# Keeping the split halves of dense weights in DRAM: a hybrid decoder layer on one Trainium2 core

## Chip, cores and metric

The kernel runs on one core of one Trainium2 chip, in one launch. The metric is device time in microseconds (us), the median of several runs. All arithmetic is in float32; TensorE's operands are in the fp32r form, a rounded float32.

## What is computed

One layer of a decoder, for a prompt of 2048 tokens and for 8 sequences of 8 new tokens each (64 rows, "the sample"), with D = 1024. Cut to what matters here:

```
ada  = silu(c) @ w_ada + b_ada                      # 6 vectors of D: shifts, scales, gates
h    = rmsnorm(x) * (1 + sc_m) + sh_m
proj = h @ w_in                                      # D x 3584
rq, rk, rv, rg, sq, sk, sv = split(proj)             # 512 columns each
ro   = retention(rotary(rq), rotary(rk), rv), normed, * silu(rg)   # 4 heads of 128
so   = stick_breaking(sq, [past k | sk], [past v | sv]), normed    # 8 heads of 64
x    = x + g_m * (concat(ro, so) @ w_out)            # 1024 x 1024
h    = rmsnorm(x) * (1 + sc_f) + sh_f
a    = h @ w_up_gate ; b = h @ w_up_val              # D x 2816 each
ff   = (silu(causal_conv3(a)) * b) @ w_down          # 2816 x D
y    = rmsnorm(x + g_f * ff)
```

The sample attends to 2048 past tokens, whose keys and values lie in pages of 128 rows, found through a page table. Outputs are y, the new keys and values, the retention states and the last rows of the convolution.

## The kernel before

**Products in halves.** A float32 operand s is written as hi + lo: hi is s rounded to fp32r, lo is the remainder. A product of two such operands is three matmuls, hi x hi, hi x lo and lo x hi (`mm3`, L293 to L297). The pair of halves is made by `split` (L173): ScalarE (ACT) casts to hi, VectorE (DVE) subtracts hi from the source. This is done for weights and for activations.

**Blocks.** The prompt goes in four blocks of 512 tokens (g = 0 to 3). Each block needs all dense weights: the input projection in `in_block` (L607), the output projection in `out_block` (L1204), the MLP in `ffn_block` (L1268). The 64 sample rows ride with block 0 in the input projection and with block 3 after it, where products are 576 columns wide, in two pieces of 288.

**Weights.** Weights come in two ways. `w_fm` (L272) loads 256 columns of all 1024 rows (1 MiB, rows of 1 KiB) into a buffer called raw, for products that leave features on the partitions; it yields two pairs of halves. `w_tm` (L288) loads four tiles of 128 rows by 512 columns (1 MiB, rows of 2 KiB) through `w_rows` (L278), for products that leave tokens on the partitions; it too yields two pairs per load. Each half is a tile whl of 128 x 1024 (512 KiB). There are two raw buffers (L241) and six whl buffers, so three pairs (L242). Every block loads and splits all weights anew: 54 loads and 102 pairs in each block, 28 pairs for the input projection, 8 for the output projection, 66 for the MLP. The modulation `ada` (L504) uses the same pools for w_ada, once: 48 pairs.

**Order.** The code is written as generators, whose steps `_weave` (L138) interleaves: first the input projection of the blocks beside the modulation's rest and the decode attention of the sample (L1463), then the last input projections beside retention and block 0's attention (L1468), then output projections and MLPs of blocks 0 to 2 beside the attention of blocks 1 to 3 (L1496), and at last block 3's MLP alone (L1499). A scheduler turns this into one list of instructions for each engine, which the engine runs in order. SyncE (SP) issues every transfer, in its own order, so a transfer whose buffer isn't free yet holds back those behind it. Among them are the decode pages (L777 to L786: a page number is read into a register, then 256 KiB are loaded), the keys, queries and values that the projections write to DRAM and the attention reads back, and the outputs.

**Tiles that the text names.** whl: halves of weights; raw: weights as loaded; act: normalised activations as features, in halves; d and z: sums in PSUM; hf: scratch rows; st, kf, vst: results on their way to DRAM; page, khl, vhl: decode pages and their halves; abe, aom, ahl: attention weights; sbr: the scale of the attention's norm. L159 is the helper `tt` (a binary operation of two tensors), L165 the helper `dma`, L174 the cast in `split`. L454 transposes the scales of the attention's norm for PE.

Of the kernel before, what the change touches and what calls it, by code (L numbers as in the profile page):

```python
# [5 lines left out]
F32 = mybir.dt.float32  # L6
F32R = mybir.dt.float32r
# [112 lines left out]
class _Stream:  # L120
    """Traced work in steps; each step yields its share of the whole, or None while it has to wait."""

# [15 lines left out]
def _weave(streams, until=None):  # L138
    """Traces the streams side by side, each at the rate that lets all of them end together."""
    while any(s.live for s in streams) and (until is None or until.live):  # L140
        for s in sorted((s for s in streams if s.live), key=lambda s: s.got / s.total):
            if s.step():
                break
        else:
            raise RuntimeError("streams wait for each other")


def body(tc, I, O):
# [18 lines left out]
    def ld(o, i):  # L167
        dma(sp, o, i)
# [7 lines left out]

    w_in, w_out = I["w_in"][0], I["w_out"][0]
    w_ug, w_uv, w_dn = I["w_up_gate"][0], I["w_up_val"][0], I["w_down"][0]
    xp = I["x_prompt"][0]
# [84 lines left out]

    # ------------------------------------------------------------ weights
    def w_split(src, a, b, eng=dve):
# [4 lines left out]

    def w_fm(src, c0):  # L272
        raw = T(wraw, [P, 2048], F32, "raw").rearrange("p (a b) -> p a b", a=8)
        ld(raw, src[:, c0 : c0 + 256].rearrange("(k p) c -> p k c", p=P))
        for m in range(2):
            yield w_split(raw[:, :, m * P : (m + 1) * P], 8, P)

# [9 lines left out]

    def w_tm(src, r0, n, c0):  # L288
        for r, raw in w_rows(src, r0, n, c0):
            for q in range(0, raw.shape[1], 2):  # L290
                yield r + q, w_split(raw[:, q : q + 2], 2, 512)

# [6 lines left out]
    def tok_mm(ps, x, w, start, stop):  # L299
        """Rows of tokens x (hi, lo) times w; a short tile has hi and lo side by side, their rows to be added."""  # L300
        if isinstance(x, tuple):
            mm3(ps, x, w, start, stop)
        else:
            pe.matmul(ps, x, w[0], start=start, stop=False)  # L304
            pe.matmul(ps, x, w[1], start=False, stop=stop)  # L305
# [40 lines left out]
    def by_tile(tiles, k0, n):  # L346
        """The products of two rows of weights with the tiles; those of the last two tile after tile."""
        order = [(k, tile) for k in range(k0, k0 + 2) for tile in tiles]
        return sorted(order, key=lambda kt: kt[1]) if k0 == n - 2 else order

    def dense_pair(wts, acts, t, features=False):
        """Two tiles of outputs, the first half of the tokens (or features) of both before the second."""
        outs = [fm_banks(t) for _ in wts]
        for h in range(2):
            for wt, out in zip(wts, outs):
                if features:
                    for ps, c0, c1 in out:
                        fm_chunk(wt, acts, ps[:, : c1 - c0], c0, c1, range(h * 4, h * 4 + 4))
                elif t == 512:
                    fm_chunk(wt, acts, out[0][0][:, h * 256 : h * 256 + 256], h * 256, h * 256 + 256)  # L360
                else:
                    ps, c0, c1 = out[h]
                    fm_chunk(wt, acts, ps[:, : c1 - c0], c0, c1)
        return outs
# [7 lines left out]

    # ------------------------------------------------------------ norms
    def rstd_of(ss, n, scale, p=P):
# [21 lines left out]
    def half_features(x, o, n, kh, A, B, acts, hpool):  # L396
        """Half kh of the columns of normalised rows, scaled and shifted, into columns o.. as hi and lo."""
        ks = slice(kh * 4, kh * 4 + 4)
# [32 lines left out]
    def sb_norm(o, n, pl, gain, tag):  # L431
        """o: [P, n], two heads of 64 rows; returns o / rms of its head * gain. Yields between its steps."""
        w = min(P, n)
# [29 lines left out]

    # ------------------------------------------------------------ preparation
    def prep(pl, kp):
# [100 lines left out]

    # ------------------------------------------------------------ input projection
    def raw_features(hp, xT):
        """The first block's rows, normalised and transposed before the modulation is known."""
        for i, o, n in TILES + [(NT, TB, NS)]:  # L570
# [179 lines left out]

    # ------------------------------------------------------------ decode attention
    def decode(dp):
# [184 lines left out]

    # ------------------------------------------------------------ retention
    def group_norm(ps, gg, qd, pl, n):
        """ps: [n, 512], four heads, each lacking its rows' decay qd; returns the gated norm of the whole."""  # L940
        mv = T(pl, [P, HR, 2], F32, "mv")
# [155 lines left out]

    # ------------------------------------------------------------ prompt attention
    def attention(blocks, tp):
# [102 lines left out]

    # ------------------------------------------------------------ output projection and MLP
    def out_block(g, xpools, fp, samp):  # L1204
        """Output projection, residual and the MLP's normalised input; xpools() gives the pool of x2."""
        t = TB + (NS if samp else 0)
# [61 lines left out]
    def ffn_block(g, x2, fp, samp, after=None):  # L1268
        """The MLP and the final norm; `after` runs between the halves of the last down projection."""
        t = TB + (NS if samp else 0)  # L1270
# [123 lines left out]
    def conv_state(fi, fp):  # L1394
        """The last rows of two tiles of gates, as rows."""
        s = T(fp, [P, 512], F32, "hf")
        ps = pz()
        for q in range(2):
            cs = T(fp, [P, 18], F32, "cvc")
            pool.tensor_copy(cs[:, 0:2], carry[:, fi + q, :])  # L1400
            pool.tensor_copy(cs[:, 2:18], scarry[:, fi + q].rearrange("p b j -> p (b j)"))
            pe.transpose(ps[:18, q * P : (q + 1) * P], cs, ident)
        act.copy(s[:18, : 2 * P], ps[:18, : 2 * P])
        cs = slice(fi * P, (fi + 2) * P)
        sv(O["conv_state_prompt"][:, cs], s[0:2, : 2 * P])
        sv(O["conv_state_sample"].rearrange("b j d -> (b j) d")[:, cs], s[2:18, : 2 * P])
# [12 lines left out]

    # ------------------------------------------------------------ the parts in their order  # L1420
    tile_pool = lambda name, bufs=1: tc.tile_pool(name=name, bufs=bufs, reuse_waits="tile")
# [85 lines left out]
class _Bufs:  # L1507
    """A pool whose tags have their own numbers of slots."""

# [9 lines left out]
class _Two:  # L1519
    """Two pools, the first for the tags given."""  # L1520

# [44 lines left out]
```

## Time and profile before

| | |
|---|---|
| median of 3 runs | 3483.96 us (3482.68 to 3484.57) |
| span of the profiled execution | 3483.6 us |
| instructions | 49,595 |
| moved by DMA | 527.72 MB, 151 GB/s on average |
| read from and written to HBM | 442.47 MB and 81.99 MB |

The profile shows one execution, so its span stands for that execution's time. PE is TensorE's matmul queue and PEld its loads of stationary weights, which overlap; a matmul's duration reaches into the next one's, since they are pipelined. A row of groups reads: line, engine, operation, tile written <- tiles read, sizes, count | busy us, mean ns of one | idle us of the engine just before, and what ended it. A row of waits reads: who waited <- for whom: us in total, times, the longest. A row of stages gives the stage, its length, the busy time of each engine with its count of instructions, the clock granted to PE, the busy share of the 16 DMA engines and the rate.

### The profile page before, as it was taken

The page shows a single profiled execution, that of the slowest core. Times are in us where ns is not written, and L with a number is a line of the kernel's source. Part 1 is how long each engine was busy: PE and PEld are TensorE (multiplying, and loading weights), DVE is VectorE, ACT ScalarE, POOL GpSimd, SP SyncE. Part 2 cuts the span into 40 slices and gives each one's busy share as a digit, 9 for nine tenths or more (in the row PEclk, how much of TensorE's full clock was granted, in tenths as well). Part 3 has the DMA queues.
Part 4 walks back from the last instruction along what each step waited for, and adds up shares of the span by engine and source line. Part 5 has one row for each costly group of instructions (what it writes and reads, how often), then busy time and mean ns, then how long its engine had stood idle before and what let it go on. Part 6 is the DMA issues. An engine that isn't in the chain of part 4 may idle for free. (4 is left out here: it accounts for less than half of the span.)

```text
span 3483.6 us, 49595 instructions
## 1 busy us (share of the span) xinstructions
PE 3298.8 (95%) x17111; PEld 2693.4 (77%) x17111; DVE 2287.1 (66%) x3258; ACT 1777.9 (51%) x3153; POOL 1021.5 (29%) x1898
## 2 busy tenths in 40 slices
PE   7999999899999989999998999998899999899998
PEld 5887877776777768777877778777677777799997
DVE  5466666665665567777768777776877775545445
ACT  5457666554544456455556555554655553433323
POOL 3012011101433243434344333333433323221113
PEclk8999999999999989999999999999999999999999
DMA  6666776666756763443453333335333334332221
GB/s 226 229 198 193 234 230 218 221 223 211 210 178 194 246 196 103 121 121 112 121 182 118 118 118 112 106 112 181 109 118 106 112 103 136 112 107 88 83 86 65
DMA packets 406233, 527.72 MB, mean 151 GB/s; under 512 B 27830, under 2 KB 244009, under 8 KB 405982
## 3 DMA queue, kind: packets, MB, share of 16 engines
q1 hardware_dynamic: 405982, 524.55, 47.8%
q8 instruction: 136, 2.23, 0.3%
q14 instruction: 115, 0.94, 0.1%
HBM read 442.47 MB, written 81.99 MB: 151 GB/s over the span
## 5 line engine op out<-in xcount | busy, mean ns | idle before, releaser
L159 DVE TENSOR_TENSOR whl<-raw,whl 128x1024 fp32r<-128x1024 f32 x456 | 572.7, 1260 | 566.8 <-ACT whl L174 556.5
L174 ACT CAST whl<-raw 128x1024 fp32r<-128x1024 f32 x456 | 477.3, 1050 | 909.2 <-PE d L296 639.0
L295 PE MATMUL d<-act,whl 128*128 128x512 f32 (+2 forms) x2016 | 741.9, 369 | 5.5 <-ACT act L424 4.7
L297 PE MATMUL d<-act,whl 128*128 128x512 f32 (+2 forms) x2016 | 737.9, 366 | 4.6 <-DVE whl L159 4.6
L296 PE MATMUL d<-act,whl 128*128 128x512 f32 (+2 forms) x2016 | 735.7, 365 | 4.2 <-POOL act L159 2.2
L295 PEld LDWEIGHTS d<-act,whl 128*128 128x128 f32 x2016 | 385.8, 192 | 66.0 <-ACT act L424 6.7
L297 PEld LDWEIGHTS d<-act,whl 128*128 128x128 f32 x2016 | 385.4, 191 | 65.0 <-DVE whl L159 5.9
L296 PEld LDWEIGHTS d<-act,whl 128*128 128x128 f32 x2016 | 387.2, 192 | 60.9 <-POOL act L159 2.6
L295 PE MATMUL d<-whl,ff 128*128 128x512 f32 x704 | 280.9, 399 | 0.0
L296 PE MATMUL d<-whl,ff 128*128 128x512 f32 x704 | 280.0, 398 | 0.0
L297 PE MATMUL d<-whl,ff 128*128 128x512 f32 x704 | 279.9, 398 | 0.0
L295 PE MATMUL d<-whl,act 128*128 128x512 f32 x640 | 258.4, 407 | 14.0 <-DVE hf L159 10.8
L296 PE MATMUL d<-whl,act 128*128 128x512 f32 x640 | 259.0, 405 | 0.1
L297 PE MATMUL d<-whl,act 128*128 128x512 f32 x640 | 257.3, 403 | 0.0
L1138 DVE TENSOR_TENSOR_SCAN aom<-aom,acy 128x512 f32<-128x512 f32 x192 | 250.9, 1307 | 5.1 <-ACT aom L1124 4.6
L159 DVE TENSOR_TENSOR abe<-abe,aom 128x512 f32<-128x512 f32 (+2 forms) x320 | 234.3, 732 | 25.9 <-POOL abe L1128 5.1
L1162 PE MATMUL acc<-ahl,avv 128*128 128x512 f32 (+3 forms) x640 | 226.0, 413 | 17.6 <-ACT ahl L174 11.4
L1124 ACT ACTIVATE aom<-z,nb 128x512 f32<-128x512 f32 (+2 forms) x320 | 201.0, 628 | 73.4 <-PE z L1121 57.2
L1121 PE MATMUL z<-akk,aq 128*128 128x512 f32 (+3 forms) x640 | 193.4, 378 | 12.0 <-DVE scd L159 5.8
L1125 ACT ACTIVATE abe<-z,bb 128x512 f32<-128x512 f32 (+2 forms) x320 | 199.7, 624 | 0.0
L159 DVE TENSOR_TENSOR ahl<-z,ahl 128x512 fp32r<-128x512 f32 (+1 forms) x320 | 191.0, 597 | 11.4 <-ACT ahl L174 11.1
L159 POOL TENSOR_TENSOR ff<-ff,hf 128x512 f32<-128x512 f32 (+1 forms) x101 | 160.5, 1611 | 107.8 <-DVE hf L159 107.7
(289 smaller groups left out, 6219.4 us busy)
## 6 DMA issues: line engine op xcount, KB each, us to landing
raw<-in_w_in SPq DMA_DIRECT2D x56, 1024.0 KB
raw<-in_w_up_gate SPq DMA_DIRECT2D x44, 1024.0 KB
raw<-in_w_up_val SPq DMA_DIRECT2D x44, 1024.0 KB
akk<-k SPq DMA_DIRECT2D x160, 256.0 KB
page<-in_cache_k_pages SPq DMA_DIRECT2D x128, 256.0 KB
page<-in_cache_v_pages SPq DMA_DIRECT2D x128, 256.0 KB
raw<-in_w_down SPq DMA_DIRECT2D x32, 1024.0 KB
raw<-in_w_ada SPq DMA_DIRECT2D x24, 1024.0 KB
```

Of the source, the lines that this page charges most:

```text
L159: eng.tensor_tensor(o, a, b, op)
L174: act.copy(hi, src)
L295: pe.matmul(ps, sh, mh, start=start, stop=False)
L296: pe.matmul(ps, sh, ml, start=False, stop=False)
L297: pe.matmul(ps, sl, mh, start=False, stop=stop)
L1121: pe.matmul(z[:, :n], qs[g, h][:, i * P : (i + 1) * P], kk[:, c, :n], start=c == 0, stop=c == 1)
L1124: act.activation(om[:, :n], z[:, :n], AF.Sigmoid, bias=nb[:, h : h + 1], scale=-SCALE)
L1125: act.activation(be[:, :n], z[:, :n], AF.Sigmoid, bias=bb[:, h : h + 1], scale=SCALE)
L1138: dve.tensor_tensor_scan(rv, rv, rv, init, ALU.mult, ALU.bypass)
L1162: pe.matmul(accs[0][:, cs], kv[u][1][:, kt, :], m[:, cs], start=(s == g and kt == 0 and c == 0), stop=(s == 0 and kt == NT - 1 and c == 1),)
```

## The change

The first time that a pair of halves of a dense weight is made, both halves are also stored to a DRAM tile of their own. When the same pair is wanted again, in a later block, the two halves are loaded straight into whl buffers; there is no raw load, no cast and no subtraction. This holds for all five dense weights: w_in, w_out, w_up_gate, w_up_val and w_down. w_ada is used once and stays as it was. Weights are named by strings, so that a pair has a key (weight, place). The numbers of buffers are the same. Comments and docstrings went as well.

```diff
+    w_in, w_out, w_ug, w_uv, w_dn = "w_in", "w_out", "w_up_gate", "w_up_val", "w_down"
+    W = {n: I[n][0] for n in (w_in, w_out, w_ug, w_uv, w_dn)}
+    KEPT = tuple(W)
+    kept = {}
...
+    def keep(key, w):
+        if key[0] in KEPT:
+            t = kept[key] = T(dram, [2, P, 1024], F32, "kw")
+            for c in range(2):
+                sv(t[c], w[c].rearrange("p a b -> p (a b)"))
+        return w
+
+    def again(key, a):
+        w = []
+        for c in range(2):
+            t = T(whl, [P, 1024], F32R, "whl")
+            ld(t, kept[key][c])
+            w.append(t.rearrange("p (a b) -> p a b", a=a))
+        return tuple(w)
+
-    def w_fm(src, c0):
+    def w_fm(name, c0):
+        keys = [(name, c0, m) for m in range(2)]
+        if keys[0] in kept:
+            for key in keys:
+                yield again(key, 8)
+            return
         raw = T(wraw, [P, 2048], F32, "raw").rearrange("p (a b) -> p a b", a=8)
-        ld(raw, src[:, c0 : c0 + 256].rearrange("(k p) c -> p k c", p=P))
-        for m in range(2):
-            yield w_split(raw[:, :, m * P : (m + 1) * P], 8, P)
+        ld(raw, W[name][:, c0 : c0 + 256].rearrange("(k p) c -> p k c", p=P))
+        for m, key in enumerate(keys):
+            yield keep(key, w_split(raw[:, :, m * P : (m + 1) * P], 8, P))
...
-    def w_tm(src, r0, n, c0):
-        for r, raw in w_rows(src, r0, n, c0):
+    def w_tm(name, r0, n, c0):
+        if (name, r0, c0) in kept:
+            for q in range(0, n, 2):
+                yield q, again((name, r0 + q, c0), 2)
+            return
+        for r, raw in w_rows(W[name], r0, n, c0):
             for q in range(0, raw.shape[1], 2):
-                yield r + q, w_split(raw[:, q : q + 2], 2, 512)
+                yield r + q, keep((name, r0 + r + q, c0), w_split(raw[:, q : q + 2], 2, 512))
```

The lines of the changed kernel below the weights' functions are 27 higher: the matmuls at L295 to L297 are at L322 to L324 there, the decode loads of L785 at L812.

More of the change, by code (lines that the diff above doesn't have):

```diff
@@ L175, in split @@
         tt(eng, lo, src, f(hi), ALU.subtract)
-    w_in, w_out = I["w_in"][0], I["w_out"][0]
-    w_ug, w_uv, w_dn = I["w_up_gate"][0], I["w_up_val"][0], I["w_down"][0]
+    w_in, w_out, w_ug, w_uv, w_dn = "w_in", "w_out", "w_up_gate", "w_up_val", "w_down"
+    W = {n: I[n][0] for n in (w_in, w_out, w_ug, w_uv, w_dn)}
+    KEPT = tuple(W)
+    kept = {}
     xp = I["x_prompt"][0]
```

## The prediction

> **What bounds the kernel now.** I read the page first (busy shares, slices, queues), then a table of stages, then the waits of PE, ACT and SP, then groups by shape, and last a few stretches of the timeline.
>
> ```profile
> PE 3298.8 (95%) x17111; PEld 2693.4 (77%) x17111; DVE 2287.1 (66%) x3258; ACT 1777.9 (51%) x3153; POOL 1021.5 (29%) x1898
> DMA  6666776666756763443453333335333334332221
> q1 hardware_dynamic: 405982, 524.55, 47.8%
> ```
>
> PE is busy for 95% of the span of 3483.6 us, so 185 us of it are idle. That is all that can be gained, since no matmul goes. The transfers come next in the first 15 slices, at 0.6 to 0.7 of the DMA engines. Block by block (the cuts lie where a block's features begin; columns: PE, PEld, DVE, ACT, POOL busy, then clock, DMA share, GB/s):
>
> ```profile
> 55.00:337.00 282.00, 271.94 (x1680) 232.01 (x1678) 159.90 (x247) 153.12 (x282) 44.40 (x92) 0.98 0.63 204
> 337.00:634.00 297.00, 281.57 (x1506) 225.73 (x1506) 193.62 (x293) 181.85 (x329) 42.42 (x88) 0.99 0.68 223
> 634.00:917.00 283.00, 266.50 (x1270) 198.95 (x1270) 168.51 (x258) 144.81 (x262) 43.20 (x89) 0.98 0.68 218
> ...
> 917.00:1340.00 423.00, 379.23 (x2106) 314.12 (x2107) 257.47 (x523) 209.20 (x419) 160.40 (x325) 0.96 0.65 195
> 1340.00:3040.00 1700.00, 1636.48 (x7674) 1306.90 (x7672) 1252.10 (x1573) 903.05 (x1536) 622.72 (x1062) 0.99 0.40 122
> 3040.00:3484.00 444.00, 427.78 (x2747) 398.64 (x2747) 222.28 (x330) 152.36 (x274) 90.44 (x208) 0.98 0.27 87
> ```
>
> The first three rows are the input projections of blocks 0, 1 and 2 with the decode attention beside them; PE idles 10, 15 and 17 us there. The next holds block 3's projection and the first output block (44 us idle), the next the MLPs beside attention (64 us), the last the MLP of block 3 alone (16 us). Does PE wait for weights? These are its waits from 917 us on, the longest first:
>
> ```profile
> PE z L454 <- POOL sbr L159: 16.9, 8, 3.0
> PE d L295 <- DVE hf L159: 11.6, 5, 4.2
> PE acc L1162 <- ACT ahl L174: 11.4, 7, 4.0
> PE z L401 <- DVE hf L159: 7.4, 6, 2.2
> ...
> PE d L297 <- DVE whl L159: 3.8, 1, 3.8
> ```
>
> Hardly: 3.8 us, once. The split halves (whl) are ready when PE comes. What PE waits for are short chains of ACT, DVE and POOL, behind which the casts and subtractions of weights may stand in the same queue.
>
> **What the change removes.** Each pair of halves costs one cast and one subtraction:
>
> ```profile
> L159 DVE TENSOR_TENSOR whl<-raw,whl 128x1024 fp32r<-128x1024 f32 x456 | 572.7, 1260 | 566.8 <-ACT whl L174 556.5 <-PE acc L1162 3.1 <-PE z L825 2.3
> L174 ACT CAST whl<-raw 128x1024 fp32r<-128x1024 f32 x456 | 477.3, 1050 | 909.2 <-PE d L296 639.0 <-PE z L304 114.1 <-PE z L296 84.7
> ```
>
> A block has 102 pairs (28 for the input projection, 74 after it), 48 of the 456 belong to the modulation. Blocks 1 to 3 lose 306 pairs: 306 x 1.26 = 386 us of DVE and 306 x 1.05 = 321 us of ACT, a sixth of either engine's work. All of it lies beside PE. It pays only where PE idles for these engines. Of the 107 us idle from 917 to 3040 us I take a fifth, a little over the share of work that goes: **-21 us** (bounds: 0, and -62, if the waits shown above, 51 us, shrink to nothing and the rest by a fifth). In blocks 1 and 2 a fifth of 32 us: **-6 us**.
>
> **What it adds on SP and the DMA engines.** SP gets 204 stores and 612 loads for 162 raw loads that go, 654 more instructions. One takes 0.39 us:
>
> ```profile
> raw<-in_w_in SPq DMA_DIRECT2D x56, 1024.0 KB
> L165 SPq DMA_DIRECT2D raw<-in_w_in x56: 368/390/715, 35.1 to 1141.9; - x56
> ```
>
> That is 255 us over the span, on an engine that mostly waits; it counts only through what stands behind it. The traffic: each pair is 1 MiB. Block 0's 28 pairs store 29.4 MB in the 282 us of the first row above, where 204 GB/s take 0.63 of the engines, so 324 GB/s would be all of them. 29.4 MB at that rate is 91 us: the share goes to about 0.95. Blocks 1 and 2 each load 29.4 MB for 14.7 MB: 45 us more in some 290, 0.68 to 0.84. The output block and MLP of block 0 store 78 MB in some 700 us, a third more on shares of 0.40 to 0.65; the later MLPs load 39 MB more each, 0.40 to about 0.6. No stage is over 1, so transfers don't set the pace by volume; they land later.
>
> **Block 0: casts behind PE.** The raw loads now share the queue with stores that wait for subtractions. The instruction order shows what this does on ACT, at the first retention columns of block 0 (raw: weights as loaded, hf: copies of a finished product's sums d and z, vst: halves of V). Before:
>
> ```order
> L174 CAST whl_1472<-raw_1470 128x1024
> L174 CAST whl_1541<-raw_1470 128x1024
> L174 CAST whl_1612<-raw_1610 128x1024
> L174 CAST vst_1441<-hf_1439 128x8x64
> L311 COPY hf_1460<-z_1258 64x512
> L174 CAST whl_1681<-raw_1610 128x1024
> L174 CAST vst_1448<-hf_1446 128x8x64
> L676 COPY hf_1463<-hf_1460 64x512
> L710 COPY hf_1527<-d_1476 64x288
> ```
>
> On ACT after, at the third and fourth pair (the first two casts stand further up):
>
> ```order
> L737 COPY hf_1572<-z_1516 64x288
> L738 COPY hf_1572<-z_1516 64x288
> L174 CAST vst_1491<-hf_1489 128x8x64
> L737 COPY hf_1638<-d_1587 64x288
> L738 COPY hf_1638<-d_1587 64x288
> L737 COPY hf_1644<-z_1588 64x288
> L738 COPY hf_1644<-z_1588 64x288
> L174 CAST whl_1654<-raw_1652 128x1024
> L174 CAST whl_1726<-raw_1652 128x1024
> ```
>
> Before, the third and fourth pair are cast ahead of the copies of the first product (d_1476). Now the third stands behind the copies of the second (d_1587), so PE, which wants it next, must wait. What a matmul takes is the step between two starts, 0.24 us; a copy takes 0.40:
>
> ```profile
> 301.27 0.40 PE L295 MATMUL d<-whl,act 128*128 128x512 f32 x1
> 301.28 0.19 PEld L296 LDWEIGHTS d<-whl,act 128*128 128x128 f32 x1
> 301.51 0.39 PE L296 MATMUL d<-whl,act 128*128 128x512 f32 x1
> ```
>
> ```profile
> L710 ACT COPY hf<-d 64x288 f32<-64x288 f32 x8 | 3.2, 396 | 9.9 <-PE d L297 9.4 <-DVE kf L159 0.3
> ```
>
> I followed each of block 0's 28 casts back to the matmul that it has to come after, and counted the matmuls from there to the pair's first use, narrower ones by their columns: before, 4 casts have fewer than ten (2.4 us), after, 14. Cast and subtraction take 2.3 us, so ten more pairs are late by up to that: **+23 us** (bounds: 0, if other matmuls fill in; 14 x (four copies of 0.40 + 2.3) = 55).
>
> **Blocks 1 and 2: halves that come late.** A load of a half may start only when its buffer is free, three pairs back; before, raw weights lay ready. How long 1 MiB takes from its issue to the cast that it releases:
>
> ```profile
> 407.92 0.39 SPq L165 DMA_DIRECT2D raw<-in_w_in  x1
> 413.02 1.05 ACT L174 CAST whl<-raw 128x1024 fp32r<-128x1024 f32 x1 [0.34 <-DMA raw<-in_w_in]
> ```
>
> 5.1 us, and a second issue of 0.39 us: 5.5 us for a pair, 23 matmuls. The order on SP at the change from V's columns to the retention queries in block 1. Before, the weights (raw_6191) go ahead of V's rows:
>
> ```order
> L165 DMA raw_6191<-in_w_in 128x8x256
> L785 ISA
> L785 DMA page_5861<-in_cache_v_pages 128x512
> L165 DMA out_v_rows_prompt<-hf_5881 128x512
> L165 DMA v_34_90<-vst_5883 128x1024
> ```
>
> After, the two halves of the pair (kw_1512 is where they lie in DRAM):
>
> ```order
> L165 DMA whl_5981<-kw_1512 128x1024
> L165 DMA v_34_90<-vst_5955 128x1024
> L812 ISA
> L812 DMA page_5949<-in_cache_v_pages 128x512
> L165 DMA out_v_rows_prompt<-hf_5960 128x512
> L165 DMA out_v_rows_prompt<-hf_5967 128x512
> L165 DMA out_v_rows_prompt<-hf_5974 128x512
> L165 DMA whl_5983<-kw_1512 128x1024
> ```
>
> The second half now stands behind the stores of all V rows, which wait for ACT's copies of the product just finished. Queued behind a waiting load are decode pages and outputs, and PE waits for the former. By the same count, 18 of the 56 pairs have fewer than 23 matmuls of room, on average some 16 (3.8 us): 18 x 1.7 = 31 us. A third I put into idle time that is there already: **+20 us** (bounds: 0, and 56 x (5.5 - 2.3) = 179, were each pair late by the difference to cast and subtraction). The output projections of blocks 1 to 3 begin with a pair loaded behind gates and residual rows, with room for 10, 18 and no matmuls: short by 3.1, 1.2 and 5.5 us, of which two thirds, **+6 us** (0 to 17, three whole loads).
>
> The Trainium skill (DMA: Bandwidth & Descriptors, Rules for kernel authors) speaks against the edit: it wants 1 MiB or more in one DMA, and halves are 512 KiB. Its fit in the section Anatomy of one DMA, which is for another issue path, gives 4.4 us for 1 MiB, an estimate; the trace's 5.1 us decides. By the fit the 18 pairs would lose 13 us less and the sum would be lower by about 8 us.
>
> **The sum:** -21 - 6 + 23 + 20 + 6 = +22 us on 3483.6 us, so **3506 us**. The profiled execution and the median of the three runs (3483.96) differ by 0.4 us. I count as no change what lies within 0.2%, 7 us, about what a measurement here can tell.
>
> **The rivals.**
>
> *Relief wins (0.27).* The order keeps PE's work nearly as it was, and three pairs of buffers may cover the late loads: in the trace ACT already waits for raw weights in blocks 1 and 2, and PE for almost none of it:
>
> ```profile
> ACT whl L174 <- DMA raw<-in_w_in: 30.5, 15, 4.5
> PE d L297 <- DVE whl L159: 0.8, 1, 0.8
> ```
>
> Then -27 stands, and with DVE's and ACT's queues shorter the POOL chain in front of L454 may give half of its 16.9 us: 3448 to 3457 us. The Trainium skill (SBUF — State Buffer, Who interferes with whom) says that a DVE instruction with two SBUF inputs blocks a POOL instruction that reads SBUF; the subtractions removed are of that kind. No row here shows POOL's instructions with and without them.
>
> *Nothing to see (0.13).* Both sides cancel, 3477 to 3491 us: PE's order sets the end and late halves fall where PE idles.
>
> *Transfers decide (0.13).* At shares of 0.84 to 0.95 each page lands behind one more half, 0.52 MB at 324 GB/s, 1.6 us. ACT waits for pages already:
>
> ```profile
> ACT vhl L174 <- DMA page<-in_cache_v_pages: 40.9, 40, 3.1
> PE z L812 <- DMA page<-in_cache_k_pages: 3.8, 5, 1.5
> ```
>
> If these 45 pass that on, it is 72 us on top of the forecast: 3578 us. It decides once the share stays above 0.9 through blocks 1 and 2. Against it: 0.84 by my count, and 4 KiB rows instead of 1 and 2 KiB ones may use the engines better.
>
> That the change doesn't do what it says I leave out: in the order every pair has its own tile in DRAM.
>
> **How the numbers follow.** The forecast's own case, 3491 to 3560 us, has 0.47. Slower is 0.47 + 0.13 = 0.60, the same 0.13, faster 0.27. The range runs from 3452 (the upper part of the relief case) to 3578 us (the transfers); it leaves out about a third of the first and half of the second.
>
> **What would show it.** Right: the window of block 0 grows by about 20 us with PE waits on whl from ACT and DVE (L295 to L305 here, L322 to L332 after); blocks 1 and 2 grow by about 7 us each with PE waits on DMA whl<-kw; from 1340 to 3040 us PE's idle time falls by some 15 us; the DMA share in block 0 exceeds 0.85. Wrong: no wait on whl<-kw over a few us in total, or blocks 0 to 2 no longer than before.

## The result, and the profile after

The changed kernel takes 3633.22 us (median of 4 runs, 3631.77 to 3637.03) against 3484.27 us for the kernel before (4 runs, 3482.68 to 3486.44): a ratio of 1.0432, 95% interval 1.0417 to 1.0447. Slower, as forecast, but by 149 us where the prediction had 22. Of three kernels below one execution each took far longer than the others (a1 7267 us, d3 4747, d5 13489) and is left out of medians and ratios.

The page of the kernel after, its busy shares, the slices of granted clock and of DMA, and the DMA queue:

```profile
PE 3352.4 (92%) x17111; PEld 2723.9 (75%) x17111; DVE 1945.8 (54%) x2952; ACT 1486.7 (41%) x2847; POOL 952.4 (26%) x1898
PEclk8999999999989998999999999999999999899999
DMA  7876777777678888777776555556565555554444
q1 hardware_dynamic: 396478, 791.98, 66.1%
```

DVE lost 341 us of work and ACT 291, nearly as counted (386 and 321). PE's busy time *rose* by 54 us for the same 17,111 matmuls, and its idle time by 93.

The stages are cut where equally many of the dense products are done. In the kernel before, blocks 0, 1 and 2 then end at 341, 638 and 922 us, a few us later than the cuts in the prediction, block 3's input and block 0's output at 1335, the MLPs beside attention at 2959. In the kernel after, these cuts lie at 391, 727, 1054, 1464 and 3113, and block 3's output projection ends at 3184. Before (blocks 0 to 2 together, then the MLPs), and after (stage by stage, then blocks 0 to 2 together):

```profile
55.00:922.00 867.00, 822.04 (x4462) 658.08 (x4461) 525.89 (x803) 483.44 (x878) 133.54 (x273) 0.98 0.67 215
1335.00:2959.00 1624.00, 1571.93 (x7395) 1257.01 (x7393) 1217.34 (x1516) 871.29 (x1473) 599.39 (x1037) 0.99 0.40 123
```

```profile
56.00:391.00 335.00, 284.09 (x1676) 236.91 (x1675) 158.49 (x244) 150.48 (x280) 44.75 (x92) 0.92 0.76 260
391.00:727.00 336.00, 297.36 (x1513) 233.17 (x1511) 162.98 (x270) 157.08 (x307) 39.92 (x89) 0.96 0.74 247
727.00:1054.00 327.00, 290.17 (x1275) 213.57 (x1274) 140.16 (x233) 120.58 (x235) 45.65 (x92) 0.91 0.72 235
1054.00:1464.00 410.00, 372.52 (x2072) 308.63 (x2072) 217.54 (x484) 177.36 (x380) 149.79 (x318) 0.96 0.83 264
1464.00:3113.00 1649.00, 1577.06 (x7395) 1263.57 (x7394) 1055.98 (x1370) 734.23 (x1330) 549.97 (x1042) 0.98 0.64 208
56.00:1054.00 998.00, 871.62 (x4460) 683.64 (x4458) 461.62 (x745) 428.14 (x820) 130.32 (x272) 0.93 0.74 247
```

Blocks 0, 1 and 2 take 335, 336 and 327 us where they took 286, 297 and 284. That is 131 of the 146 us by which the span grew. In them the mean DMA share is 0.72 to 0.76, no more, and the clock fell from 0.98 to 0.93: 872 us of PE busy time instead of 822, and 126 us idle instead of 45. PE's longest waits there, and a shorter one, then one of ACT's, from the waits of blocks 0 to 2:

```profile
PE d L322 <- ACT whl L174: 22.7, 6, 12.1
PE z L428 <- DVE hf L159: 17.5, 7, 5.9
PE d L322 <- DMA whl<-kw: 9.8, 10, 4.0
PE acc L912 <- ACT vhl L174: 8.6, 12, 2.0
PE d L324 <- DMA whl<-kw: 7.6, 7, 2.8
PE z L839 <- DMA page<-in_cache_k_pages: 6.6, 8, 1.5
```

```profile
ACT vhl L174 <- DMA page<-in_cache_v_pages: 111.5, 63, 7.1
```

PE waits for casts, for the normalised rows (L428 transposes them) and for halves. What it waits for keys and values of the decode has grown little, from 11 us to 15 (8.6 and 6.6; before, 3.8 and the row below), while ACT waits for value pages for 111.5 us where it was 40.9.

```profile
PE acc L885 <- ACT vhl L174: 7.2, 11, 1.3
```

The longest stall of block 0, on PE, ACT and SP (idle time in front, and what ended it, in brackets; ACT's rows begin with the norm of block 1's rows):

```profile
329.66 1.22 PE L322 MATMUL d<-whl,act 128*128 128x512 f32 x2 [12.05 <-ACT whl L174]
```

```profile
317.79 0.64 ACT L411 ACTIVATE hf<-xt 128x512 f32<-128x512 f32 x1
...
327.52 1.15 ACT L631 ACTIVATE vst<-vst,rs_b 128x1024 f32<-128x1024 f32 x1 [1.21 <-POOL rs_b L159]
328.57 1.03 ACT L174 CAST whl<-raw 128x1024 fp32r<-128x1024 f32 x1
```

```profile
316.99 0.44 SPq L165 DMA_DIRECT2D raw<-in_w_in  x1
```

Two things are late at once. The raw load is issued at 317.0, when PE runs out of work; and its cast stands on ACT behind the whole norm of the next block, 10 us of it. Is that the order, the queue, or the bytes? The profile can't tell; the experiments can.

### The profile page after: what moved, and what is told of

Its sections match the earlier page's. It is cut to its first block, busy times and chain, and to the rows that moved or that the text cites. A ratio compares the mean times of both kernels' runs of the same rounds, so it can differ in the third digit from the quotient of the medians.

```text
span 3630.1 us, 49877 instructions
## 1 busy us (share of the span) xinstructions
PE 3352.4 (92%) x17111; PEld 2723.9 (75%) x17111; DVE 1945.8 (54%) x2952; ACT 1486.7 (41%) x2847; POOL 952.4 (26%) x1898
## 5 line engine op out<-in xcount | busy, mean ns | idle before, releaser
L322 PE MATMUL d<-act,whl 128*128 128x512 f32 (+2 forms) x2016 | 746.1, 371 | 18.0 <-ACT whl L174 9.0
L324 PE MATMUL d<-act,whl 128*128 128x512 f32 (+2 forms) x2016 | 740.5, 368 | 9.4 <-DMA whl<-kw 8.3
L322 PEld LDWEIGHTS d<-act,whl 128*128 128x128 f32 x2016 | 387.3, 192 | 81.3 <-ACT whl L174 10.8
L324 PEld LDWEIGHTS d<-act,whl 128*128 128x128 f32 x2016 | 386.3, 192 | 75.2 <-DMA whl<-kw 12.7
L174 ACT CAST ahl<-z 128x512 fp32r<-128x512 f32 (+1 forms) x320 | 167.2, 523 | 410.7 <-PE z L1177 405.6
L322 PE MATMUL d<-whl,act 128*128 128x512 f32 x640 | 251.4, 413 | 36.6 <-issue 16.2
L322 PE MATMUL d<-whl,ff 128*128 128x512 f32 x704 | 280.9, 399 | 0.0
L324 PE MATMUL d<-whl,ff 128*128 128x512 f32 x704 | 280.6, 399 | 0.0
L159 DVE TENSOR_TENSOR whl<-raw,whl 128x1024 fp32r<-128x1024 f32 x150 | 187.7, 1260 | 150.6 <-ACT whl L174 142.7
L324 PE MATMUL d<-whl,act 128*128 128x512 f32 x640 | 258.2, 403 | 0.0
L1322 DVE SCALAR_TENSOR_TENSOR c<-a,vecs,c 128x512 f32<-128x512 f32 x176 | 134.2, 763 | 213.2 <-ACT c L1319 162.9
L174 ACT CAST whl<-raw 128x1024 fp32r<-128x1024 f32 x150 | 155.8, 1049 | 217.7 <-PE d L323 178.3
L159 DVE TENSOR_TENSOR hf<-d,gp 128x512 f32<-128x512 f32 x160 | 108.4, 684 | 178.6 <-PE d L324 158.5
```

The lines of the kernel that those rows point to most:

```text
L159: eng.tensor_tensor(o, a, b, op)
L174: act.copy(hi, src)
L322: pe.matmul(ps, sh, mh, start=start, stop=False)
L324: pe.matmul(ps, sl, mh, start=False, stop=stop)
L1322: dve.scalar_tensor_tensor(c[:, :TB], a[:, j : j + TB], cw(j), c[:, :TB], ALU.mult, ALU.add)
```

## The experiments

The first theory was that the loss lies in blocks 0 to 2 and comes of SP standing at stores that wait. Times in the table are microseconds more than before in each stage (one profiled execution each); medians are of all executions but the three named above, and the ratios are to runs of the kernel before on the same chip (their medians lie between 3478 and 3484 us). Executions of one kernel lie up to 31 us apart (c3: 3587 to 3618), and the profiled one of c3 is 17 us under its median, that of a7 13 above, so a difference of some 10 us between two rows tells little.

| kernel | blocks 0, 1, 2 | block 3 in, block 0 out | MLPs by attention | rest | median | ratio (95%) |
|---|---|---|---|---|---|---|
| the change | +50 +38 +44 | -3 | +24 | -7 | 3633 | 1.043 |
| a1: MLP and output only | -2 -2 -2 | +11 | +21 | -7 | 3505 | 1.008 (1.005 to 1.011) |
| a2: input only | +54 +40 +43 | -12 | -3 | -1 | 3604 | 1.034 (1.032 to 1.036) |
| a3: stores alone, all blocks | +54 +86 +89 | +48 | -4 | 0 | 3760 | 1.080 (1.078 to 1.082) |
| a4: loads alone | +6 +35 +51 | -13 | -1 | -3 | 3554 | 1.020 (1.017 to 1.022) |
| a5: resident pair | +8 -10 -6 | -23 | -24 | -11 | 3421 | 0.984 (0.982 to 0.985) |
| a6: a3, stores of a constant | +62 +94 +91 | +50 | -1 | -6 | 3780 | 1.087 (1.085 to 1.089) |
| a7: a3, stores on POOL | +46 +47 +43 | 0 | 0 | -3 | 3604 | 1.035 (1.033 to 1.037) |
| a8: a4, loads on POOL | +7 +58 +42 | -15 | -4 | 0 | 3578 | 1.030 (1.027 to 1.032) |
| c1: a3, old order | +50 +66 +60 | +9 | -1 | -5 | 3665 | 1.054 (1.051 to 1.056) |
| c2: no stores, a3's order | +48 +88 +82 | +48 | +5 | -4 | 3743 | 1.075 (1.073 to 1.077) |
| c3: the change, old order | +51 +35 +25 | +2 | -6 | -4 | 3604 | 1.037 (1.034 to 1.040) |
| d1: a6, old order | +46 +44 +59 | +8 | -3 | -4 | 3626 | 1.041 (1.038 to 1.043) |
| d2: a7, old order | +43 +43 +37 | +6 | -4 | -4 | 3606 | 1.034 (1.031 to 1.038) |
| d3: the change on POOL, old order | +39 +39 +38 | -2 | -20 | +1 | 3583 | 1.030 (1.026 to 1.034) |
| d5: a1, old order | +1 -1 -2 | +15 | -8 | -3 | 3487 | 1.001 (1.000 to 1.003) |
| e1: d2 with an eighth of the bytes | -1 +2 +9 | +6 | -1 | +2 | 3499 | 1.006 (1.004 to 1.007) |
| e2: a1 on POOL | +1 -1 +3 | +7 | -8 | -7 | 3475 | 0.998 (0.997 to 1.000) |
| e3: a1 on POOL, old order | -5 -1 +2 | +9 | -19 | -2 | 3475 | 0.999 (0.997 to 1.000) |

"Old order" is the order of the kernel before, on all five engines.

**Which weights (a1, a2).**

```diff
-    KEPT = tuple(W)
+    KEPT = (w_out, w_ug, w_uv, w_dn)      # a1
+    KEPT = (w_in,)                        # a2
```

> Only the weights of the output projection and the MLP are kept; the input projection loads and splits its raw weights in every block, as before the change. Theory (the loss is made in blocks 0 to 2, by halves and raw weights whose DMAs are issued late because they stand in SP's queue behind waiting ones, and by TensorE's clock falling after the stalls): blocks 0, 1 and 2 take as long as before, within 5 us each; block 3's input with block 0's output 0, the MLPs beside attention +3, the output projection of block 3 +15, the last MLP -2: 3484 + 16 = 3500 us. Rival 'the added bytes cost time anywhere': the MLP part carries 222 of the 306 pairs that are loaded again, so some 70% of the 149 us stays: 3590 us. Rival 'the relief is real and was hidden by the late start of the later stages': 3457 us.

> Only the input projection's weights are kept; those of the output projection and the MLP are loaded raw and split in every block, as before the change. Theory (the loss is made in blocks 0 to 2): +43, +39 and +48 us there, the rest as before: 3484 + 130 = 3614 us. Rival 'the added bytes cost time anywhere': 84 of 306 pairs, 30% of 149 us: 3530 us.

The two parts come apart: some 20 us with the MLP's weights, 222 of the 306 pairs that are loaded again, and 120 with the input projection's 84. Pair for pair, those beside the decode cost far more.

**Stores alone, loads alone (a3, a4).** a3 drops the entry in `kept`, so the halves are stored and never read; a4 lets every later pair read the first pair's tile.

```diff
-            t = kept[key] = T(dram, [2, P, 1024], F32, "kw")
+            t = T(dram, [2, P, 1024], F32, "kw")              # a3
...
+            kept[key] = one[0]                                # a4, stored at the first key only
```

> The 28 pairs of block 0's input projection are stored in DRAM and never read; all later blocks load and split raw weights as before the change, and nothing else is kept. Theory (stores that wait for subtractions hold back the raw loads behind them in SP's queue): block 0 loses its 43 us and blocks 1 and 2 nothing: 3527 us. Rival 'block 0's delay of the decode attention and of ACT's queue is carried into blocks 1 and 2': 3570 to 3614 us. Rival 'the stores themselves cost nothing, loads make the loss': 3484 us within 7.

> Of the input projection only the very first pair is stored, and every pair of blocks 1 to 3 loads this one again in place of its own halves (other weights, the same bytes and the same instructions); nothing else is kept. Theory (loads of halves that are issued late make the loss of blocks 1 and 2 by themselves): block 0 as before, blocks 1 and 2 +39 and +48 us: 3571 us. Rival 'blocks 1 and 2 lose because of what block 0's stores have shifted': 3484 us within 10. Rival 'transfers': loads of twice the bytes without any stores in DRAM cost a share of their own, but the two blocks are at 0.73 of the DMA engines in the changed kernel, so this would show as a share above 0.9 there.

a3's expectation describes it wrongly: with no entry in `kept`, every block splits and stores its 28 pairs, 117 MB in all, not block 0 alone. So its 276 us are four blocks of stores, and block 0's +54 is the part that answers to the theory. a4 puts the loss of blocks 1 and 2 on the loads by themselves (+86 us), with no store before them, or on the new order that comes with the loads; no run held the order still with loads alone. In block 3, where no decode pages are loaded any more, the same loads *gain* 13 us.

**The relief by itself (a5).** One pair stays in SBUF and serves all later blocks; its room comes from the buffers of halves, four in place of six.

```diff
-            t = T(whl, [P, 1024], F32R, "whl")
-            ld(t, kept[key][c])
+        return tuple(t.rearrange("p (a b) -> p a b", a=a) for t in kept[key])   # the one pair
```

> The relief by itself: blocks 1 to 3 neither load nor split weights but use one pair that stays in SBUF (wrong weights, the same matmuls), no halves are stored, and the room for that pair comes from four buffers of halves in place of six. Theory (PE's idle time after block 0 belongs to chains of ACT, DVE and POOL in which the splits hardly stand; two earlier kernels gained 9 to 12 us in block 3's input with block 0's output and nothing beside the MLPs): blocks 1 and 2 -5 each, then -12, then 0: about -20 from block 1 on. Rival 'the relief is large and was eaten by late loads': -27 to -60 from block 1 on, with at least -15 of it beside the MLPs. Block 0 with four buffers may lose some 0 to 30 us in both; it is read apart.

Here theory fell and rival won, beyond its own range: some 74 us from block 1 on, 24 of them beside the MLPs. The relief is there; in the changed kernel something eats it.

**Is it SP waiting at stores? (a6, a7, a8)**

```diff
-                sv(t[c], w[c].rearrange("p a b -> p (a b)"))
+                sv(t[c].rearrange("p (a b) -> p a b", a=2), fixed.to_broadcast([P, 2, 512]))   # a6
+                dma(pool, t[c], w[c].rearrange("p a b -> p (a b)"))                            # a7
...
-            ld(t, kept[key][c])
+            dma(pool, t, kept[key][c])                                                         # a8
```

> As the kernel that stores the input projection's halves in every block and never reads them (3760 us), but what is stored is a fixed tile of constants: the same number of stores, the same bytes (rows of 2 KiB in place of 4), the same place in SP's queue, and no wait for a cast or subtraction and no buffer of halves held. Theory (the loss comes of SP standing at stores that wait for a subtraction, with raw weights, pages and other stores behind them): 3484 to 3500 us. Rival 'bytes or the ring of the queue': 3700 us or more, since nothing of the transfers changes.

> As the kernel that stores the input projection's halves in every block and never reads them (3760 us), with these stores issued from POOL's queue in place of SP's. Theory (SP's order): SP no longer stands at them: 3484 to 3530 us, the rest of it POOL's own work behind the waiting stores. Rival 'a half's buffer is held until its store has landed, some 4 to 5 us after the subtraction, so casts wait for buffers': stays at 3700 us or more, and ACT's and DVE's waits for the kw stores show it.

> As the kernel in which blocks 1 to 3 load one stored pair again and again (3554 us), with these loads issued from POOL's queue in place of SP's. Theory (SP's order): a load is issued when its buffer is free and POOL reaches it, so most of the 70 us of blocks 1 and 2 goes: 3484 to 3510 us. Rival 'three pairs of buffers are too few for a load that starts only when its buffer is free': 3540 us or more, with PE waiting for the loads.

The first theory falls. Stores that wait for nothing cost as much (a6), and loads on another queue cost more (a8). The rival of too few buffers isn't seen in a8 either: PE waits 15 us there for its halves, 19 in a4. a7 leaves 125 of a3's 276 us, between the two forecasts. But all three have a new instruction order too, for the scheduler works the order out anew. By the lists used below, the fewest rows that have to move to turn the order of before into a3's are some 1,000 of PE's 16,670 and 310 of ACT's 3,050. No comparison so far has held the order still.

**Holding the order still (c1, c2, c3).** Each engine's instructions are recorded as they are written, and tied to a list taken from another kernel by edges that set the order and wait for nothing. With the stores and loads of halves left out of the list, the rows of PE, ACT, DVE, POOL and SP are then those of the other kernel.

```diff
+    for e, order in _order().items():
+        insts = [log[e][k] for k in order]
+        insts = [i for i in insts if i is not None]
+        for i, j in zip(insts, insts[1:]):
+            tc.add_manual_dep(j, i.name, ...)         # NoSync: j behind i on its engine
```

> The kernel that stores the input projection's halves in every block and never reads them (3760 us), with every engine's instructions tied to the order that they have in the kernel before; only the 224 stores are free to stand anywhere on SP. Bytes, stores and buffers stay. The first theory (SP standing at stores that wait for a subtraction) fell, since stores of a constant cost as much. New theory (the loss is in the order: the scheduler works with its own times for transfers, and with the stores in its sums it puts raw loads later on SP, casts later on ACT, and other work ahead of them): most of the 276 us goes, 3484 to 3530 us. Rival 'bytes, in the DMA engines or in the order of SP's queue': 3700 us or more.

> The counterpart: the kernel before, with no store of any half, with every engine's instructions tied to the order that they have in the kernel that stores the input projection's halves in every block (3760 us). New theory (the order makes the loss): 3650 to 3750 us with not one byte added. Rival 'bytes': 3484 us within 15, since nothing is added.

> The whole change, with all work that the two kernels share tied to the order of the kernel before on all five engines; the stores and loads of halves alone are free to stand anywhere on SP. New theory (the order makes the loss, the change itself relieves ACT and DVE): 3420 to 3490 us, faster than the changed kernel by some 150 us or more. Rival 'loads that wait for one of six buffers come late whatever the order': blocks 1 and 2 keep at least half of their 39 and 48 us: 3530 us or more. Rival 'bytes': 3600 us or more.

Theory and rival are both half right. The order alone, with not a byte added, costs 265 us (c2). And the stores, with the old order, still cost 187 (c1). Either is enough, and together they make 276, not the sum. For the whole change the theory fell: c3 was to take 3420 to 3490 us and takes 3604. What PE waits for in blocks 0 to 2 differs: of c2 (line numbers of these kernels are a few higher than in their models),

```profile
PE d L298 <- ACT whl L177: 68.8, 23, 12.1
PE acc L888 <- ACT vhl L177: 27.6, 19, 8.2
PE z L815 <- DMA page<-in_cache_k_pages: 17.8, 9, 7.5
```

the casts behind other work, as in the stall shown; of c1, PE's and then SP's,

```profile
PE z L844 <- DMA page<-in_cache_k_pages: 52.0, 18, 8.1
PE acc L917 <- ACT vhl L177: 42.9, 20, 8.1
```

```profile
SPq L168 <- ACT whl L177: 69.9, 28, 9.3
SPq L817 <- PE z L844: 50.1, 39, 5.1
SPq L817 <- DVE vhl L162: 48.6, 33, 4.9
SPq L168 <- DVE whl L162: 38.8, 39, 3.8
```

the decode pages, with SP standing 109 us at casts and subtractions of weights, whose stores it now issues. Before, it stood 23 us at them, nearly all in this row:

```profile
SPq L165 <- DVE whl L159: 21.1, 9, 4.3
```

**Queue or bytes (d1, d2, d3, d5).** All under the old order; edits as in a6, a7, a7 with a8 for the whole change, and a1.

> As the kernel that stores the input projection's halves in every block under the old order (3665 us, 187 above the kernel before), but what is stored is a fixed tile of constants, so that no store waits for a cast or a subtraction; the stores are free to stand anywhere on SP. Theory (under the old order the loss is SP standing at stores that wait, with pages behind them): 3480 to 3520 us. Rival 'bytes in the DMA engines': 3620 us or more.

> As the kernel that stores the input projection's halves in every block under the old order (3665 us), with the stores issued from POOL's queue; SP's order is word for word that of the kernel before. Theory (SP standing at stores): 3480 to 3530 us. Rival 'bytes': 3620 us or more. Rival 'buffers of halves held until the store has landed': 3550 us or more with ACT waiting for the stores.

> The whole change under the old order, with the stores and the loads of halves issued from POOL's queue. Theory (order and SP's queue make the loss): block 0 within 10 us of before, blocks 1 and 2 within 10 each, later stages -10 to -40: 3440 to 3490 us. Rival 'six buffers are too few for loads of 5 us': blocks 1 and 2 keep 25 us each or more: 3510 us or more. Rival 'POOL's own work behind waiting loads': the MLP stages lose, PE waits for POOL.

> Under the old order, only the weights of the output projection and the MLP are kept, with stores and loads on SP; the input projection splits raw weights in every block, as before the change. Theory: blocks 0 to 2 as before; the relief shows beside the MLPs once the order is held, -5 to -25 us there: 3455 to 3475 us. Rival 'late loads eat it': 3478 us within 7 or above.

d1 doesn't answer its question. Stores that wait for nothing may stand anywhere, and the scheduler put them in bursts: the four longest stalls of PE add up to 115 us, of 143 lost. The worst, on SP and ACT, and that stretch of the stages:

```profile
739.09 50.77 SPq L168 DMA_DIRECT2D kw<-con  x38
789.97 1.26 SPq L168 DMA_DIRECT2D xt<-in_x_prompt  x1
791.47 1.01 SPq L818 DMA_DIRECT2D page<-in_cache_v_pages  x1
```

```profile
796.50 0.62 ACT L177 CAST vhl<-page 128x512 fp32r<-128x512 f32 x1 [55.19 <-DMA page<-in_cache_v_pages]
```

```profile
739.00:790.00 51.00, 8.66 (x64) 7.41 (x63) 2.33 (x3) 2.29 (x5) 1.81 (x1) 0.62 1.03 382
```

The DMA engines are full here, at 382 GB/s.

d2 does answer: with SP's rows as before and the stores off SP, 123 us stay. So 64 of c1's 187 us came of SP's queue: SP standing at the stores, the issue of 224 of them at 0.33 us each, and their place ahead of pages. No run parts these three. Buffers held until a store has landed aren't the rest: in blocks 0 to 2 ACT never waits for a store of halves, and DVE once, for 1.2 us. Blocks 0 to 2 of d2, then their waits:

```profile
55.00:383.00 328.00, 285.26 (x1679) 241.16 (x1680) 163.53 (x251) 156.83 (x289) 75.88 (x152) 0.93 0.79 274
383.00:723.00 340.00, 296.60 (x1505) 234.28 (x1505) 192.88 (x292) 181.03 (x327) 71.61 (x144) 0.94 0.81 281
723.00:1044.00 321.00, 281.25 (x1272) 206.26 (x1272) 170.01 (x261) 146.94 (x264) 75.30 (x148) 0.94 0.83 284
```

```profile
PE acc L917 <- ACT vhl L177: 36.9, 24, 4.9
PE z L844 <- DMA page<-in_cache_k_pages: 31.9, 19, 5.5
```

PE waits 69 us for keys and values of the decode where it was 11. Counting the bytes landed on SP's queue against those issued, I estimate that a page of blocks 0 to 2 takes 3.1 us (median; 95 of 100 under 7.0) where it took 2.3 (4.4). The mean share of the DMA engines hides what it meets. Cut into pieces of 5 us, blocks 0 to 2 have the engines over 0.95 busy in 9% of the pieces before, in 39% of d2's.

d3 was to take 3440 to 3490 us and misses that too: +116 in blocks 0 to 2 with order and SP out of the question, 29% of the pieces over 0.95 and pages at 2.8 us (7.9), and now the relief beside the MLPs, -20. Its blocks 1 and 2 lose more than the 25 us each that the rival of too few buffers asked for, but PE waits 51 us for what depends on pages there and only 12.5 for halves:

```profile
PE z L848 <- DMA page<-in_cache_k_pages: 30.6, 13, 5.5
PE acc L921 <- ACT vhl L177: 20.7, 17, 4.1
PE d L331 <- DMA whl<-kw: 9.1, 3, 5.0
```

d5's relief is smaller with stores and loads on SP, -8, and block 0's output pays +15 for its stores.

**Bytes (e1), and a kernel without the loss (e2, e3).** e2 is a1 with stores and loads on POOL; e3 is e2 under the old order.

```diff
-                dma(pool, t[c], w[c].rearrange("p a b -> p (a b)"))
+                dma(pool, t[c, 0:16], w[c].rearrange("p a b -> p (a b)")[0:16])    # e1, of d2
```

> As the kernel that stores the input projection's halves in every block from POOL's queue under the old order (3605 us, 123 above the kernel before), with only 16 of the 128 partitions of each half stored: the same instructions, waits and buffers, an eighth of the bytes (15 MB in place of 117). Theory (what is left under the old order is bytes: pages and raw weights that land later): 3483 + 123/8 = 3498 us, 3480 to 3510. Rival 'the instructions on POOL, their waits or the buffers held': 3580 us or more.

> Only the weights of the output projection and the MLP are kept, with their stores and loads on POOL's queue, the order left to the scheduler. Theory (DMA engines are 0.4 busy beside the MLPs, so the bytes fit there, and the relief of ACT and DVE shows): -20 us beside the MLPs, block 0's output 0 to +10: 3465 to 3480 us. Rival 'a new order costs as much again, as on SP': 3490 to 3510 us.

> The same under the order of the kernel before. Theory: blocks 0 to 2 within 3 us of before, -20 us beside the MLPs as in the kernel with the whole change on POOL: 3460 to 3470 us. Rival 'the stores of block 0's output and MLP cost what they cost on SP (+15 us)': 3475 to 3485 us.

With the same instructions, waits and buffers, an eighth of the bytes leaves 20 of 123 us, near the 15 that goes by bytes. The waits of d2 are gone:

```profile
PE acc L917 <- ACT vhl L177: 8.8, 12, 1.4
PE z L844 <- DMA page<-in_cache_k_pages: 5.3, 9, 1.6
```

A page takes 2.6 us (4.6) by the same count, and 14% of the pieces are over 0.95. So some 100 of d2's 123 us go with the stores' bytes. That the loads' bytes cost as much wasn't tried by itself. e2 and e3 keep the bytes away from the decode and off SP: 0.998 (0.997 to 0.9995) and 0.9985 (0.9974 to 0.9996), some 4 us faster than before by the medians. Of the versions that compute the whole layer these are the fastest, and it is close to nothing: e2 gains 8 us beside the MLPs, where 20 were expected; e3 gains 19 and gives 9 back to the stores of block 0's output.

## Why the prediction was wrong, point by point

By the experiments the 149 us are made of three causes, peeled off one by one: some 100 us remain with order and SP taken out (d3, after its relief); stores and loads on SP add some 25 (c3); the new order adds some 23 (the change). The last two are known to some 15 us each, from the intervals of the ratios. That d3's 100 us are bytes is shown for stores (e1) and argued for loads, from d3's waits for pages. Nor are the parts additive, as c1 and c2 show: PE, ACT, SP and the decode pages wait for one another in a ring there, and whoever is late makes the rest late. In the change itself the lateness reaches PE more through casts and halves than through pages.

- **"No stage is over 1, so transfers don't set the pace by volume; they land later."** This is the step that failed. The volume was right (29.4 MB a block), the conclusion wrong, and with it the sum, which has no term for what other transfers lose by landing later. A stage needs no mean share of 1 for bytes to cost: at means of 0.72 to 0.83 the blocks of the change and of d2 lost some 40 us each, and d3, with order and SP out of the question, is still 100 us slower than before. The mean hides that single pieces of 5 us are full more often (over 0.95 in 9% of them before, 18% in the change, 29% in d3, 39% in d2). Two sizes were off as well: the forecast shares of 0.95 and 0.84 came from 204 GB/s at 0.63, 324 for all engines; the burst of d1 moves 382 at a share of 1.03. And the blocks grew longer, which lowers the share.

  The rival "transfers decide" had much of the mechanism, 3578 us and a chance of 0.13; its condition, a mean share above 0.9, was wrong, and so was "decides". Its 72 us for pages that pass on a late landing compare with 58 more on PE's waits in d2. That ACT's wait for value pages grew by 71 us in the change is luck: by the estimate above pages land 2.5 us after their issue there (95 of 100 under 4.2), hardly later than before, so it is their issue that came late.
- **Block 0, +23.** Measured +50. The mechanism, casts ordered behind copies and then the norm, is real: c2, in a3's order, loses 48 without any store. But with the old order the stores make +51 (c3) and +39 from POOL (d3), so undoing the order would not have helped. The upper bound, 55, held, by luck as much as by its reasons, since it counted late casts alone.
- **Blocks 1 and 2, +20.** Measured +82. The count of pairs with little room explains the waits for halves, 17 us on PE in the rows of blocks 0 to 2, about as much as forecast. What it named and gave no price is what stands behind the loads and beside them: pages. In block 3, where pages are gone, the same loads cost nothing (a4, -13).
- **The clock.** No term of the sum had it. Counted in the trace's clock records, PE ran at half clock for 34 us in blocks 0 to 2 before and for 142 after; PE's busy time there grew by 50 us with the same matmuls. So of the 131 us 50 are clock and 81 idle time. Each microsecond of new stall cost 0.6 more.
- **Relief, -27.** Of -21 from block 3's input on nothing is left (-3 and +24), and beside the MLPs PE's idle time rose from 52 to 72 us where I wanted some 15 less. By itself it is larger than I took it: some 74 us from block 1 on (a5), 24 beside the MLPs. With the halves' transfers on POOL 20 of these 24 remain (d3), on SP 8 (d5), and with the scheduler's order there is +24, 16 of which are the next point.
- **Output projections, +6 (0 to 17).** One stall, at block 3, measured 16.2, the longest of all. The place was right, halves behind gates and residual rows; the price was not one load but SP's own stand at the gates (gp), ahead of both (PE's wait, then SP's rows):

```profile
PE d L322 <- issue: 16.2, 1, 16.2
```

```profile
3087.62 0.52 SPq L165 DMA_DIRECT2D act<-mx  x1
3095.55 0.33 SPq L165 DMA_DIRECT2D gp<-gp  x1
3095.93 0.42 SPq L165 DMA_DIRECT2D smp<-ms  x1
3096.41 1.85 SPq L165 DMA_DIRECT2D ff<-in_x_prompt  x4
3098.30 0.64 SPq L165 DMA_DIRECT2D ff<-in_x_sample  x1
3098.98 5.33 SPq L165 DMA_DIRECT2D whl<-kw  x6
```

SP stands for 7.4 us, and the halves are issued from 3099.0 on, 11 us after the first of these rows ended.

Open: what the loads' bytes cost by themselves, since no run made the loads small under the old order. Open too: how much of the new order's harm in the changed kernel is the raw load's late issue on SP and how much the cast's place on ACT. Tying one engine at a time would tell; it wasn't tried. Nor was a decode with more page buffers.

## What to carry to other kernels

Before adding traffic to a stage, ask which small transfers in it have little slack (here 256 KiB pages with three buffers), and price how much later these land; a mean share of the DMA engines under 1 doesn't say that it is nothing. An edit that a scheduler sees changes the order on every engine, and that can cost more than the edit: to know which it was, tie the order and run both halves, the edit without its order and the order without its edit. And add the clock: in this kernel, where PE is all but always busy, new stalls of some microseconds were paid about one and a half times.

## What the runs showed of the hardware

- The clock falls after short stalls. In the clock records PE runs at 1.0 or at 0.5, in pieces of 3.41 us and multiples of it (3.41, 6.83, 10.24); in the changed kernel's blocks 0 to 2 the longest stall that touched the 3.41 us ahead of a fall has a median of 1.9 us (22 falls). Of some 220 pieces of 3.41 us at full clock there that no fall follows, 3 are touched by a stall as long. The Trainium skill (TensorE: Matmul & The Clock Gate, Part 1: The HAM clock gate) states the two levels and the window of 3.4 us, and the trace agrees; in the section HAM oscillation it gives as the rule no gaps over about 3.4 us, and here shorter ones were enough.
- SP is held when much is queued. In d1 38 stores of 512 KiB in a row occupy it for 50.77 us, 1.34 us each, with the DMA engines full (a share of 1.03), where the quickest of the 224 such stores is issued in 0.52; a page issued 52 us after the burst began ended a wait of 55.19 us on ACT.
- Another issuing engine doesn't make room. 224 stores moved from SP to POOL (c1 to d2) save 64 us of 187; 123 stay. The Trainium skill (DMA: Bandwidth & Descriptors, Issuing engines are not separate DMA queues) says that all issuers share the same 16 DMA engines; the 123 us agree. Whether the 64 saved are the issue itself (224 times 0.33 us) or SP's standing and the order in its queue, no run shows.
